# Multi-query attention on one core: score rounds planned by tiles that come free on the way, 27 weight places, two copies of V

## Chip, cores and metric

The kernel runs on one core of one Trainium2 chip. The metric is the time of one execution on the device in microseconds. A core has TensorE (PE; its weight loads are PEld), VectorE (DVE), ScalarE (ACT), GpSimd (POOL) and SyncE (SP), each with its own queue, which work beside each other and wait for one another through semaphores.

## What is computed

```python
q: (8, 1024, 16, 64)   k, v: (8, 1024, 64)   # batch, sequence, heads, head_dim
scores = q @ k^T / sqrt(64)                  # per batch and head; k and v are shared by the heads
weights = exp(scores - max); weights /= sum(weights)
out = weights @ v                            # (8, 1024, 16, 64)
```

## The kernel before

The work is cut into 1024 units of scores. A unit is 128 keys by two heads by 512 queries: two matmuls with 64 rows each (line 263), which write one of three score tiles in PSUM (two banks each). The scores lie with the keys on the partitions, so that the weights can be the stationary operand of the second product. A unit's number u runs over pairs of heads (64, eight in each batch), in each over two halves of the queries, and in each over eight blocks of keys.

Each unit is exponentiated in one of two ways. `kinds[u]` says in which:

- "A": ScalarE's exponential reads the score tile and writes 16-bit weights into one of N_WT places (line 276).
- "V": VectorE does it in passes over one of N_W3 triple places. `ve_bits` (line 283) reads the score tile and writes 16-bit integers that, read as 16-bit floats, are a first approximation. `ve_mantissa` (294), `ve_power` (304) and `ve_square` (315) make a mantissa, a power of two and a square from them, and a product of two of these is the third term. That product is shared: GpSimd takes the first columns of it, often in one or two pieces (`ve_cube`, line 319), and VectorE the rest (`ve_rest`, line 327). GpSimd's pieces are put beside passes of VectorE that read PSUM.

The value matmuls (line 396) multiply 128x128 blocks of weights with 65 columns of V (64 and one of ones, which gives the sum). An "A" unit needs eight, one for each of its 128x128 blocks; a "V" unit needs 24, since it has three terms, each with its own copy of V scaled by a coefficient (`vp`, three copies for each of two batches; `prep_v`, line 251, makes the scaled ones). Seven results share one of two PSUM banks; when they are complete VectorE takes the reciprocal of the sums (`inverse`, line 345) and multiplies (`finish`, line 354), and SyncE's queue stores them. q comes through GpSimd's DMA queue (line 166) as 16-bit and is turned by DMA transposes on SyncE's queue; the first q tiles are turned on TensorE.

All of this is ordered ahead of time by a planner, `plan()`, which runs on the host when the kernel is built. It keeps a clock for TensorE (`t_pe`), VectorE (`t_ve`), ScalarE (`t_act`) and GpSimd (`t_gp`), in nanoseconds, from constants such as T_PAIR (one unit of scores), T_MM (one value matmul), T_IN and T_OUT (going to scores and back), T_ACT and VE_COST. What it emits is only an order of instructions on each engine: the times in it bind nothing on the chip. There each engine goes through its own queue in order and waits for what its next instruction needs.

Scores are issued in rounds: TensorE does some units of scores, then value matmuls until the next round. `plan()` counts the score tiles that are free (`n_free`). If there are two or more it starts a round of so many. If there is one, it starts a round of one only where waiting for the next tile would leave ScalarE without work (`WAIT`, `NEAR`). `issue()` decides whether a unit goes to VectorE: only the second unit of a round may (`VSLOT = 1`), if VectorE's backlog is below `VE_SLACK`, the unit before did not go there, and the number of V units so far is below a share `RATE` of the units. `SAFE` is a margin that the planner adds to the time at which weights are ready before it orders their value matmul; `REST` is how many columns of the product may be left for VectorE; `LATE` and `NEXT` decide between VectorE's next passes.

Of the kernel before, what the change touches and what calls it, by code (L numbers as in the profile page):

```python
# [10 lines left out]
FP32 = mybir.dt.float32  # L11
FP16 = mybir.dt.float16
I32 = mybir.dt.int32
I16 = mybir.dt.int16
ALU = mybir.AluOpType
# [3 lines left out]

SUM_LO = 128.0  # L20
SUM_HI = 60000.0
C0 = 0.9833984375
C3 = 0.163818359375
CS = 2.1471603163479376
N_WT = 22
N_W3 = 8
N_M = 2
N_M2 = 3
T_PAIR = 214.0
T_IN = 96.0  # L30
T_OUT = 106.0
T_MM = 29.6
T_SCORE = 480.0
T_ACT = 917.0
ACT_DONE = 1110.0
MM_DONE = 270.0
VE_TAIL = 115.0
# [17 lines left out]
    "finish": 542.0,  # L55
}
ORDER = {"bits": 0, "inverse": 1, "finish": 2}
NEXT = {"bits": 0.0, "inverse": 0.0, "finish": 0.0}
MINC = 128
REST = 768  # L60
LATE = 500.0
VSLOT = 1
DEFER = 12
HOLD = 1400.0
VE_SLACK = 2500.0
V_END = 12
RATE = 0.235
NEAR = 2000.0
WAIT = -100.0
T_BITS = 1255.0  # L70
SAFE = 300.0


@with_exitstack
def attention_main(ctx, tc, q, k, v, out, flag):
# [13 lines left out]
    P = 128  # L89
    NKT = S // P  # L90
    QCH = 512
# [12 lines left out]
    consts = ctx.enter_context(tc.tile_pool(name="consts", bufs=1))  # L104
# [3 lines left out]
    wtp = ctx.enter_context(tc.tile_pool(name="wtp", bufs=1))  # L108
# [8 lines left out]
    ident16 = consts.tile([P, P], FP16, name="ident16")  # L117
    ones = consts.tile([P, 1], FP32, name="ones")
    rec_all = consts.tile([P, NG], FP32, name="rec_all")
    vps = [consts.tile([P, 3, NKT, 72], FP16, name=f"vp{i}") for i in range(2)]  # L120
    ok_all = consts.tile([P, B + GRP], FP32, name="ok_all")
    qf = consts.tile([P, NKT, P], FP32, name="qf")

    sc = {}
    ve = {}
# [3 lines left out]
    q16 = {}  # L129
# [21 lines left out]
        )  # L151

    def load_q_first(p):
        q16[("first", p)] = consts.tile([P, NKT, P], FP16, name=f"q16_first{p}")
        src = q[0, :, 2 * p : 2 * p + 2, :].rearrange("(c p) h d -> p c (h d)", p=P)
        if p:
            nc.gpsimd.dma_start(out=q16[("first", p)], in_=src)
            return
        for cs in (slice(0, NKT // 2), slice(NKT // 2, NKT)):
            nc.scalar.dma_start(out=qf[:, cs, :], in_=src[:, cs, :])  # L160
# [86 lines left out]

    def prep_v(b):
        vp = kv[b]["vp"]
        for i, ci in ((1, C0), (2, C3)):  # L250
            x = nc.vector.tensor_scalar(  # L251
                out=vp[:, i, :, 0:D], in0=vp[:, 0, :, 0:D], scalar1=ci, scalar2=None, op0=ALU.mult
            )
        return x
# [23 lines left out]
    def ve_bits(u, i):  # L278
        p, c, j = where(u)
        w3 = w3p.tile([P, 3, 2, QCH], FP16, tag=f"w3_{i}", name=f"we{p}_{c}_{j}")  # L280
        wt[u] = [(w3[:, 1], 0), (w3[:, 0], 1), (w3[:, 2], 2)]
        ve[u] = {"w3": w3}
        nc.vector.tensor_scalar(  # L283
            out=w3[:, 1].bitcast(I16),
            in0=sc.pop(u),
            scalar1=15.0 * 1024,
            scalar2=0.0,
            op0=ALU.add,
            op1=ALU.max,
        )  # L290

    def ve_mantissa(u, i):
        ve[u]["m"] = mp.tile([P, 2, QCH], FP16, tag=f"m{i}", name=f"m{u}")
        return nc.vector.tensor_scalar(  # L294
            out=ve[u]["m"].bitcast(I16),
            in0=ve[u]["w3"][:, 1].bitcast(I16),
            scalar1=0x3FF,
            scalar2=0x3C00,
            op0=ALU.bitwise_and,
            op1=ALU.bitwise_or,  # L300
        )

    def ve_power(u):
        return nc.vector.tensor_scalar(  # L304
            out=ve[u]["w3"][:, 0].bitcast(I16),
            in0=ve[u]["w3"][:, 1].bitcast(I16),
            scalar1=0x7C00,
            scalar2=None,
            op0=ALU.bitwise_and,
        )  # L310

    def ve_square(u, i):
# [154 lines left out]
    def plan():  # L467
        ops = []

        def emit(t, what, *args):  # L470
            ops.append((t, len(ops), what, args))

        t_pe = t_ve = t_act = t_gp = 0.0
        mode = "v"
        u = 0
        free = [0.0] * 3
# [31 lines left out]
        def slot():  # L508
            return min(range(3), key=lambda i: free[i])
# [7 lines left out]
        def backlog():  # L517

            t = sum(VE_COST[k] for k, _ in chain) + VE_COST["rest"] * len(left)
            return t + sum(VE_COST[k] for _, k, _, _ in evict)  # L520
# [24 lines left out]
        def vector_step(limit):  # L545
# [21 lines left out]
            if not urgent and (  # L567
                chain or left and (flush or left[next(iter(left))] <= REST or u - next(iter(left)) > DEFER)
            ):
                what, v = chain[0] if chain else ("rest", next(iter(left)))  # L570
                old = next(iter(left), None)
                if old is not None and (
                    left[old] <= REST
                    or what == "square"
                    and min(m2_used) == float("inf")
                    or u - old > DEFER
                ):
                    what, v = "rest", old
                s = t_ve
                if what == "mantissa":  # L580
                    s = max(s, ready[v, 0], min(m_used))
                elif what == "square":
                    s = max(s, live["s", v], min(m2_used))
                elif what == "rest":
                    s = max(s, squared[v] + VE_TAIL)
                if s >= limit:
                    return False
                share(s)
                s = max(s, lock)
                if what == "rest":  # L590
                    n = left.pop(v)
                    done = 0.0
                    if n:
                        emit(s, "rest", v, 2 * QCH - n)
                        t_ve = s + VE_FIX + n / 1.92
                        done = t_ve + VE_TAIL
                        behind, t_behind = ("rest", v), t_ve
                    ready[v, 2] = m2_used[live.pop(("m2", v))] = max(done, ready.get((v, "g"), 0.0))
                    return True
                chain.pop(0)  # L600
                t_ve = s + VE_COST[what]
                if what in ("prep_k", "prep_v", "check"):
                    emit(s, what, v)
                    behind, t_behind = (what, v), t_ve
                    return True
                done = t_ve + VE_TAIL
                behind, t_behind = (what, v), t_ve
                if what == "mantissa":
                    live["m", v] = hold(m_used, s)[0]
                    live["s", v] = done  # L610
                    emit(s, what, v, live["m", v])
                elif what == "power":
                    emit(s, what, v)
                    ready[v, 1] = done
                else:
                    m_used[live.pop(("m", v))] = done
                    live["m2", v] = hold(m2_used, s)[0]
                    emit(s, what, v, live["m2", v])
                    left[v] = 2 * QCH
                    squared[v] = t_ve  # L620
                return True
# [24 lines left out]
                    chain.append(("check", b))  # L646
            return True

        def issue(t, first):
            nonlocal u, t_act, made_v  # L650
            i = slot()
            s = max(t, free[i])
            to_v = (
                first
                and NKT <= u < STEPS - V_END
                and not todo
                and max(t_ve, s) + backlog() < s + T_SCORE + VE_SLACK
                and kinds.get(u - 1) != "V"
                and made_v < (u - NKT + 1) * RATE
                and min(w3_used) < s  # L660
            )
            if not to_v and min(wt_used) == float("inf"):
                return False
            kinds[u] = "V" if to_v else "A"
            made_v += to_v
            emit(s, "score", u, i)
            done = s + T_SCORE
            free[i] = float("inf")
            if to_v:
# [26 lines left out]
        while h < H or u < STEPS:  # L696
# [2 lines left out]

            while vector_step(t_pe):  # L700
                pass
            n_free = sum(f <= t_pe for f in free)
            go = n_free > 1
            if n_free == 1:
                other = sorted(late_free(i) for i in range(3))[1]
                go = max(other, t_pe) + T_IN + T_SCORE > t_act + WAIT and t_pe + NEAR >= t_act - T_IN - T_SCORE
            if u < STEPS and go:
                t = t_pe + (T_IN if mode == "v" else 0)
                k = 0
                while u < STEPS and k < n_free and issue(t, n_free > 1 and k == VSLOT):  # L710
                    t += T_PAIR
                    k += 1
                if k:
                    rounds += mode == "v"
                    mode = "s"
                    t_pe = t
                    continue
# [63 lines left out]
    with tc.manual_schedule():  # L781
# [6 lines left out]
        for c in range(NKT):  # L788
            load_q(0, c)
        for t in vps:  # L790
            for i, ci in enumerate((1.0, C0, C3)):
                nc.gpsimd.memset(t[:, i, :, D : D + 1], ci)
        nc.vector.tensor_copy(out=ident16, in_=ident)
        nc.vector.memset(ones, 1.0)
# [166 lines left out]
```

## Time and profile before

| | |
|---|---|
| time, median of 3 runs | 763.24 us (762.63 to 763.75) |
| the profiled execution's own time | 762.94 us |
| its span, from the first to the last instruction | 761.1 us |
| mean granted TensorE clock | 0.997 |
| units on ScalarE / on VectorE | 800 / 224 |
| value matmuls in the main loop | 11,712 |
| pieces of the product on GpSimd | 279 |

The span is what the profile's rows add up to; the profiled execution's own time is 1.84 us longer. In the profile, "Lnnn" is a line of the kernel. Names such as `sc`, `wt`, `we`, `ot` are tiles: scores, ScalarE's weights, VectorE's weights, results. A group's row has the number of its instructions, the time in which at least one of them ran, the mean length of one in ns, and the idle time of the engine in front of them. Records of instructions that follow each other on one engine overlap, so the mean length of one is more than its distance to the next.

### The profile page before, as it was taken

How to read it: one execution, taken by the hardware profiler on the slowest of the kernel's cores; microseconds unless marked ns; L12 is line 12 of the kernel's file. 1: busy time of each engine (PE TensorE's matmuls, PEld its weight loads, DVE VectorE, ACT ScalarE, POOL GpSimd, SP SyncE). 2: the span in 40 equal slices, each digit the busy share in tenths (PEclk: the TensorE clock that was granted, in tenths of full speed). 3: DMA queues.
4: the chain of work that ended last, by engine and by line, in shares of the span. 5: the costliest groups of instructions: out<-in, count | busy, mean ns of one | idle time of the engine just before them, and what ended most of it. 6: DMA issues, size and time to landing. Idle time of an engine off the chain costs nothing.

```text
span 761.1 us, 31746 instructions
## 1 busy us (share of the span) xinstructions
PE 746.3 (98%) x13858; PEld 480.7 (63%) x13858; DVE 728.8 (96%) x1474; ACT 747.5 (98%) x803; POOL 327.2 (43%) x364
## 2 busy tenths in 40 slices
PE   6999999999999999999999999999999999999996
PEld 3566666666666666666666666666666665666665
DVE  4999999999999999999999999999999999999994
ACT  7999999999999999999999999999999999999995
POOL 4644444443444344543444344434444334444440
PEclk9999999999999999999999999999999999999999
DMA  9964437663466525665446563467535565211112
GB/s 173 167 121 99 99 64 114 113 117 94 78 118 113 105 62 112 106 113 92 79 93 112 114 113 74 90 111 125 99 75 95 100 112 96 71 44 58 30 58 73
DMA packets 168926, 73.91 MB, mean 97 GB/s; under 512 B 94032, under 2 KB 161616, under 8 KB 168784
## 3 DMA queue, kind: packets, MB, share of 16 engines
q1 hardware_dynamic: 149152, 53.76, 32.7%
q0 software_dynamic: 18576, 17.57, 18.3%
q8 instruction: 109, 1.79, 1.1%
q10 hardware_dynamic: 1056, 0.52, 0.2%
q14 instruction: 33, 0.27, 0.1%
HBM read 37.75 MB, written 33.55 MB: 94 GB/s over the span
## 4 chain that ended last, share of the span: by engine, by line
ACT 54%; PE 42%; issue 3%; DMA 1%; DVE 1%
ACT wt L276 54%; PE ot L396 24%; PE sc L263 17%; DMA knat<-in_k_dram 0%; PE otl L420 0%; DMA out_dram<-osb 0%; DVE osb L354 0%; PE kps L200 0%; PE qps L216 0%; DVE k L191 0%; DVE rec_all L345 0%; DVE k2t L212 0%; PE cnt L837 0%; DVE okm L835 0%; DVE ok_all L443 0%
## 5 line engine op out<-in xcount | busy, mean ns | idle before, releaser
L276 ACT ACTIVATE wt<-sc 128x1024 f16<-128x1024 f32 x800 | 745.0, 1046 | 1.1 <-PE sc L263 0.9
L319 POOL TENSOR_TENSOR we<-we,mm 128x448 f16<-128x448 f16 (+4 forms) x279 | 281.9, 1010 | 409.2 <-DVE mm L315 214.4
L396 PE MATMUL ot<-vp,wt 128*128 128x65 f16 x6336 | 432.2, 194 | 0.0
L396 PE MATMUL ot<-vp,we 128*128 128x65 f16 x5376 | 432.2, 194 | 0.0
L396 PEld LDWEIGHTS <-wt 128*128 128x128 f16 x6336 | 317.4, 97 | 115.0 <-issue 115.0
L396 PEld LDWEIGHTS <-we 128*128 128x128 f16 x5376 | 316.1, 97 | 104.5 <-issue 103.4
L263 PE MATMUL sc<-qt,k2t 64*128 64x512 f16 x2048 | 354.3, 385 | 4.4 <-ACT wt L276 2.9
L283 DVE TENSOR_SCALAR we<-sc 128x1024 int16<-128x1024 f32 x224 | 272.5, 1217 | 8.7 <-PE sc L263 6.7
L315 DVE TENSOR_TENSOR mm<-m 128x1024 f16<-128x1024 f16 x224 | 151.8, 678 | 0.0
L263 PEld LDWEIGHTS <-k2t 64*128 64x128 f16 x2048 | 80.1, 93 | 48.5 <-issue 7.8
L294 DVE TENSOR_SCALAR m<-we 128x1024 int16<-128x1024 int16 x224 | 92.5, 413 | 0.2
L304 DVE TENSOR_SCALAR we<-we 128x1024 int16<-128x1024 int16 x224 | 92.5, 413 | 0.0
L354 DVE TENSOR_TENSOR osb<-ot,rec_all 128x448 f32<-128x448 f32 x146 | 89.2, 611 | 0.2
L327 DVE TENSOR_TENSOR we<-we,mm 128x576 f16<-128x576 f16 (+7 forms) x222 | 87.4, 394 | 0.0
L166 POOL DMA_DIRECT2D q<-in_q_dram x64 | 38.6, 606 | 5.5 <-issue 1.5
L345 DVE RECIPROCAL rec_all<-ot 128x7 f32<-128x7 f32 x146 | 28.7, 197 | 7.4 <-PE ot L396 6.8
L149 POOL DMA_DIRECT2D vp<-in_v_dram x8 | 7.2, 899 | 0.0
L251 DVE TENSOR_SCALAR vp<-vp 128x512 f16<-128x512 f16 x16 | 3.8, 279 | 2.2 <-DMA vp<-in_v_dram 2.2
L200 PE MATMUL kps<-ident,k 128*64 128x128 f16 x16 | 1.3, 314 | 4.4 <-DVE k L191 4.3
L234 DVE TENSOR_SCALAR k16d<-knat 128x1024 f16<-128x1024 f32 x7 | 4.7, 672 | 0.0
L229 DVE COPY qt<-qps 128x512 f16<-128x512 f16 (+1 forms) x2 | 1.1, 555 | 3.0 <-PE qps L216 3.0
L200 PEld LDWEIGHTS <-k 128*64 128x64 f16 x16 | 0.8, 158 | 4.6 <-DVE k L191 4.6
(30 smaller groups left out, 23.7 us busy)
## 6 DMA issues: line engine op xcount, KB each, us to landing
out_dram<-osb SPq DMA_DIRECT2D x109, 256.0 KB, 2.6
q<-in_q_dram POOLq DMA_DIRECT2D x56, 256.0 KB, 4.4
out_dram<-osb SPq DMA_DIRECT2D x38, 128.0 KB, 2.4
knat<-in_k_dram SPq DMA_DIRECT2D x7, 256.0 KB, 3.9
q<-in_q_dram POOLq DMA_DIRECT2D x8, 192.0 KB, 8.2
vp<-in_v_dram POOLq DMA_DIRECT2D x8, 128.0 KB, 5.8
qt<-q SPq DMA_TRANSPOSE x64, 4.8
qf<-in_q_dram ACTq DMA_DIRECT2D x2, 256.0 KB, 4.0
```

Source lines behind the costliest of these rows:

```text
L166: nc.gpsimd.dma_start(out=q16[(b, c)], in_=q[b, c * P : (c + 1) * P, h0:, :].rearrange("p h d -> p (h d)"),)
L263: nc.tensor.matmul(sc[u][:, hh, :], k2t[r : r + 64, j * P : (j + 1) * P], qt[b][r : r + 64, p % HP, c * QCH : (c + 1) * QCH], start=True, ...
L276: nc.scalar.activation(out=w, in_=sc.pop(u), func=EXP, scale=escale, bias=math.log(CS))
L283: nc.vector.tensor_scalar(out=w3[:, 1].bitcast(I16), in0=sc.pop(u), scalar1=15.0 * 1024, scalar2=0.0, op0=ALU.add, op1=ALU.max,)
L294: return nc.vector.tensor_scalar(out=ve[u]["m"].bitcast(I16), in0=ve[u]["w3"][:, 1].bitcast(I16), scalar1=0x3FF, scalar2=0x3C00, op0=ALU.b ...
L304: return nc.vector.tensor_scalar(out=ve[u]["w3"][:, 0].bitcast(I16), in0=ve[u]["w3"][:, 1].bitcast(I16), scalar1=0x7C00, scalar2=None, op0 ...
L315: return nc.vector.tensor_tensor(out=ve[u]["m2"], in0=m, in1=m, op=ALU.mult)
L319: x = nc.gpsimd.tensor_tensor(out=wu[:, lo:hi], in0=we[:, lo:hi], in1=mm[:, lo:hi], op=ALU.mult)
L327: return nc.vector.tensor_tensor(out=wu[:, lo:], in0=we[:, lo:], in1=mm[:, lo:], op=ALU.mult)
L345: nc.vector.reciprocal(out=rec_all[:, g0 : g0 + n], in_=o[:, 0:n, D])
L354: nc.vector.tensor_tensor(out=ob[:, i0 : i0 + n, :], in0=o[:, 0:n, 0:D], in1=rec.unsqueeze(2).broadcast_to([P, n, D]), op=ALU.mult,)
L396: nc.tensor.matmul(ots[g0][:, gg - g0, 0 : D + 1], w[:, hh, qb * P : (qb + 1) * P], kv[h // (HP * NCH)]["vp"][:, ci, u % NKT, 0 : D + 1], ...
```

## The change

The reference computation stays the same. VectorE's approximation gets other constants: its three terms need two copies of V, plain and times KAPPA, in place of three. The first q tiles, which had places of their own, now lie in places of the rings that are used late, and N_WT goes from 22 to 27. The planner's constants change, and its rule for rounds:

- A tile counts as free if it will be so when TensorE gets to it: the first at once (`FIRST`), the next by `t_in + n_free * T_PAIR + SOON`.
- In a round of two or more the unit for VectorE may be the first, where ScalarE does not need its unit at once (`at_v`).
- With one tile free, a round of one unit may go to VectorE alone, where ScalarE has work for over `AWAY` ns and VectorE's backlog is below `SLACK1`.

```diff
-C0 = 0.9833984375
-C3 = 0.163818359375
-CS = 2.1471603163479376
-N_WT = 22
+KAPPA = 1.5258396029178207
+CS = 3.2766468288976904
+N_WT = 27
-T_PAIR = 214.0
+T_PAIR = 215.5
-T_OUT = 106.0
-T_MM = 29.6
+T_OUT = 120.0
+T_MM = 30.2
-T_ACT = 917.0
+T_ACT = 905.0
-NEXT = {"bits": 0.0, "inverse": 0.0, "finish": 0.0}
+NEXT = {"bits": 100.0, "inverse": 0.0, "finish": 60.0}
-REST = 768
-LATE = 500.0
-VSLOT = 1
+REST = 500
+LATE = 2500.0
+EPS = 0.0
+AWAY = 1500.0
+SLACK1 = 300.0
+SOON = 0.0
+FIRST = 0.0
-VE_SLACK = 2500.0
+VE_SLACK = 1800.0
-RATE = 0.235
+RATE = 0.25
-WAIT = -100.0
+WAIT = 0.0
-SAFE = 300.0
+SAFE = 1000.0
...
-    vps = [consts.tile([P, 3, NKT, 72], FP16, name=f"vp{i}") for i in range(2)]
+    vps = [consts.tile([P, 2, NKT, 72], FP16, name=f"vp{i}") for i in range(2)]
-    qf = consts.tile([P, NKT, P], FP32, name="qf")
+    qf = (w3p.tile([P, 3, 2, QCH], FP16, tag=f"w3_{N_W3 - 1}", name="qf") ...)
...
-        q16[("first", p)] = consts.tile([P, NKT, P], FP16, name=f"q16_first{p}")
+        x = wtp.tile([P, 2, QCH], FP16, tag=f"wt{N_WT - 1 - p}", name=f"q16_first{p}")
+        q16[("first", p)] = x.rearrange("p h (c f) -> p (h c) f", f=P)
...
     def prep_v(b):
-        for i, ci in ((1, C0), (2, C3)):
+        for i, ci in ((1, KAPPA),):
...
     def ve_bits(u, i):
-        wt[u] = [(w3[:, 1], 0), (w3[:, 0], 1), (w3[:, 2], 2)]
+        wt[u] = [(w3[:, 1], 1), (w3[:, 0], 0), (w3[:, 2], 0)]
...
     def ve_mantissa(u, i):
-            scalar2=0x3C00,
+            scalar2=0x3800,
...
     def ve_power(u):
             scalar1=0x7C00,
-            scalar2=None,
+            scalar2=0x0201,
             op0=ALU.bitwise_and,
+            op1=ALU.bitwise_or,
...
-        def issue(t, first):
-            to_v = (
-                first
-                and NKT <= u < STEPS - V_END
+        def wants(s, slack):
+            return (
+                NKT <= u < STEPS - V_END
                 and not todo
-                and max(t_ve, s) + backlog() < s + T_SCORE + VE_SLACK
+                and max(t_ve, s) + backlog() < s + T_SCORE + slack
                 and kinds.get(u - 1) != "V"
                 and made_v < (u - NKT + 1) * RATE
                 and min(w3_used) < s
             )
+        def issue(t, slack):
+            to_v = slack is not None and wants(s, slack)
...
-            n_free = sum(f <= t_pe for f in free)
+            t_in = t_pe + (T_IN if mode == "v" else 0.0)
+            n_free = 0
+            for f in sorted(free):
+                if f > (t_in + n_free * T_PAIR + SOON if n_free else t_pe + FIRST):
+                    break
+                n_free += 1
             go = n_free > 1
+            slack = VE_SLACK if go else None
             if n_free == 1:
                 other = sorted(late_free(i) for i in range(3))[1]
                 go = max(other, t_pe) + T_IN + T_SCORE > t_act + WAIT and t_pe + NEAR >= t_act - T_IN - T_SCORE
+                if t_act > t_in + AWAY and wants(t_in, SLACK1):
+                    go = True
+                    slack = SLACK1
             if u < STEPS and go:
-                t = t_pe + (T_IN if mode == "v" else 0)
+                t = t_in
                 k = 0
-                while u < STEPS and k < n_free and issue(t, n_free > 1 and k == VSLOT):
-                    t += T_PAIR
+                at_v = int(n_free > 1 and t + T_PAIR + T_SCORE > t_act + EPS)
+                while u < STEPS and k < n_free and issue(t, slack if k == at_v else None):
+                    t = t_now + T_PAIR
                     k += 1
```

More of the change, by code (lines that the diff above doesn't have):

```diff
@@ L119, in attention_main @@
     rec_all = consts.tile([P, NG], FP32, name="rec_all")
-    vps = [consts.tile([P, 3, NKT, 72], FP16, name=f"vp{i}") for i in range(2)]
+    vps = [consts.tile([P, 2, NKT, 72], FP16, name=f"vp{i}") for i in range(2)]
     ok_all = consts.tile([P, B + GRP], FP32, name="ok_all")
-    qf = consts.tile([P, NKT, P], FP32, name="qf")
+    qf = (
+        w3p.tile([P, 3, 2, QCH], FP16, tag=f"w3_{N_W3 - 1}", name="qf")
+        .rearrange("p i h q -> p (i h q)")[:, 0 : 2 * NKT * P]
+        .bitcast(FP32)
+        .rearrange("p (c f) -> p c f", f=P)
+    )
     sc = {}
@@ L471, in emit @@
             ops.append((t, len(ops), what, args))
-        t_pe = t_ve = t_act = t_gp = 0.0
+        t_pe = t_ve = t_act = t_gp = t_now = 0.0
         mode = "v"
@@ L597, in vector_step @@
                         behind, t_behind = ("rest", v), t_ve
-                    ready[v, 2] = m2_used[live.pop(("m2", v))] = max(done, ready.get((v, "g"), 0.0))
+                    done = max(done, ready.get((v, "g"), 0.0), ready[v, 1])
+                    m2_used[live.pop(("m2", v))] = done
+                    ready[v, 2] = done
                     return True
@@ L647, in vector_step @@
             return True
-        def issue(t, first):
-            nonlocal u, t_act, made_v
-            i = slot()
-            s = max(t, free[i])
-            to_v = (
-                first
-                and NKT <= u < STEPS - V_END
+        def wants(s, slack):
+            return (
+                NKT <= u < STEPS - V_END
                 and not todo
-                and max(t_ve, s) + backlog() < s + T_SCORE + VE_SLACK
+                and max(t_ve, s) + backlog() < s + T_SCORE + slack
                 and kinds.get(u - 1) != "V"
@@ L661, in issue @@
             )
+        def issue(t, slack):
+            nonlocal u, t_act, made_v, t_now
+            i = slot()
+            s = max(t, free[i])
+            to_v = slack is not None and wants(s, slack)
             if not to_v and min(wt_used) == float("inf"):
@@ L664, in issue @@
             kinds[u] = "V" if to_v else "A"
-            made_v += to_v
+            if to_v:
+                made_v += 1
             emit(s, "score", u, i)
+            t_now = s
             done = s + T_SCORE
@@ L790, in attention_main @@
         for t in vps:
-            for i, ci in enumerate((1.0, C0, C3)):
+            for i, ci in enumerate((1.0, KAPPA)):
                 nc.gpsimd.memset(t[:, i, :, D : D + 1], ci)
```

## The prediction

> **What bounds the kernel now.** I read the engine line and the chain of the page first, then the busy time by stretches.
>
> ```profile
> PE 746.3 (98%) x13858; PEld 480.7 (63%) x13858; DVE 728.8 (96%) x1474; ACT 747.5 (98%) x803; POOL 327.2 (43%) x364
> ...
> ACT 54%; PE 42%; issue 3%; DMA 1%; DVE 1%
> ```
> ```profile
> 0.00:20.00 20.00, 13.77 (x139) 6.85 (x140) 9.37 (x22) 15.26 (x17) 9.67 (x25) 0.91 1.21 174
> ...
> 300.00:400.00 100.00, 99.88 (x1882) 64.81 (x1880) 98.43 (x200) 100.00 (x109) 43.52 (x48) 1.00 0.56 100
> ...
> 740.00:761.10 21.10, 15.18 (x360) 11.71 (x356) 11.01 (x32) 12.39 (x14) 1.58 (x2) 0.96 0.23 66
> ```
>
> The columns of the stretches are length, then busy time of PE, PEld, DVE, ACT, POOL, then clock, DMA share and GB/s. Three engines are over 98% busy in the middle. A busy ACT or PE may still be waiting, because instructions overlap in the records; the chain, which passes between ACT and PE, is the first hint. So I ask what each engine needs when it waits for nobody, ScalarE first.
>
> ```profile
> L276 ACT ACTIVATE wt<-sc 128x1024 f16<-128x1024 f32 x800 | 745.0, 1046 | 1.1 <-PE sc L263 0.9
> ```
> ```profile
> L276 ACT ACTIVATE wt<-sc x800: 1018/1023/1236, 7.0 to 751.3; 128x1024 f16<-128x1024 f32 x160
> ```
> ```profile
> 14.67 12.61 ACT wt L276 x14
> ...
> 97.81 4.56 ACT wt L276 x5
> ...
> 145.22 3.74 ACT wt L276 x4
> ```
>
> The starts of the 800 exponentials run from 7.0 to 751.3 us, one every (751.3 - 7.0) / 799 = 0.931 us. The last three rows are pieces of the chain. The longest has 14 in 12.61 us, 0.901 each; the others 0.912 and 0.935. ScalarE alone would need 800 x 0.901 = 721 us where it takes 745. Some 24 us are waits, shorter than the overlap of two records (1.046 - 0.931 = 0.115 us), so that the waits view does not see them.
>
> TensorE next: the timeline (start and length in us, count at the end), a line of the waits (us in total, times, longest) and the groups.
>
> ```profile
> 300.46 0.39 PE L263 MATMUL sc<-qt,k2t 64*128 64x512 f16 x2
> ...
> 300.78 0.27 PE L396 MATMUL ot<-vp,wt 128*128 128x65 f16 x3
> ...
> 301.27 0.20 PE L396 MATMUL ot<-vp,we 128*128 128x65 f16 x1
> ...
> 301.40 0.39 PE L263 MATMUL sc<-qt,k2t 64*128 64x512 f16 x2
> ...
> 302.35 0.61 PE L263 MATMUL sc<-qt,k2t 64*128 64x512 f16 x4
> ...
> 302.89 0.24 PE L396 MATMUL ot<-vp,wt 128*128 128x65 f16 x2
> ...
> 304.12 0.19 PE L396 MATMUL ot<-vp,wt 128*128 128x65 f16 x1
> ...
> 304.24 0.61 PE L263 MATMUL sc<-qt,k2t 64*128 64x512 f16 x4
> ```
> ```profile
> PEld L396 <- issue: 218.4, 740, 0.4
> ```
> ```profile
> L396 PE MATMUL ot<-vp,wt 128*128 128x65 f16 x6336 | 432.2, 194 | 0.0
> L396 PE MATMUL ot<-vp,we 128*128 128x65 f16 x5376 | 432.2, 194 | 0.0
> L263 PE MATMUL sc<-qt,k2t 64*128 64x512 f16 x2048 | 354.3, 385 | 4.4 <-ACT wt L276 2.9 <-DVE we L283 0.8
> ```
>
> A score unit is two of these matmuls. Between the rounds that start at 300.46 and 301.40 lie one unit and 17 value matmuls (the L396 rows between, of which the first and the last are shown, added up), in 0.94 us; from 302.35 to 304.24 two units and 41, in 1.89 us. A further unit costs 0.61 - 0.39 = 0.22. So a value matmul costs (1.89 - 0.94 - 0.22) / 24 = 0.030 us, and what is left of the first, 0.94 - 0.22 - 17 x 0.030 = 0.20 us, is paid per round: going from value matmuls to scores and back. The waits view has 740 such returns. Counted through the trace by its score rows there are 744 rounds: 475 of one unit, 264 of two, 4 of three and one long one at the start. Sum for TensorE: 1024 x 0.22 = 225, 11,712 x 0.0305 = 357, 744 x 0.20 = 149, together 731 of the 745 us of the exponentials; rounding and the start hold the rest. It idles 4.4 us in front of scores. So **TensorE is the pacemaker**, and a fifth of its time is the changing between two kinds of matmul. ScalarE's hidden waits are waits for it.
>
> VectorE, one full cycle from its timeline:
>
> ```profile
> 299.88 0.67 DVE L315 TENSOR_TENSOR mm<-m 128x1024 f16<-128x1024 f16 x1
> ...
> 300.48 1.21 DVE L283 TENSOR_SCALAR we<-sc 128x1024 int16<-128x1024 f32 x1
> ...
> 301.62 0.19 DVE L345 RECIPROCAL rec_all<-ot 128x7 f32<-128x7 f32 x1
> ...
> 301.73 0.41 DVE L294 TENSOR_SCALAR m<-we 128x1024 int16<-128x1024 int16 x1
> ...
> 302.06 0.61 DVE L354 TENSOR_TENSOR osb<-ot,rec_all 128x448 f32<-128x448 f32 x1
> ...
> 302.59 0.34 DVE L327 TENSOR_TENSOR we<-we,mm 128x384 f16<-128x384 f16 x1
> ...
> 302.86 0.41 DVE L304 TENSOR_SCALAR we<-we 128x1024 int16<-128x1024 int16 x1
> ...
> 303.19 0.68 DVE L315 TENSOR_TENSOR mm<-m 128x1024 f16<-128x1024 f16 x1
> ```
> ```profile
> DVE we L283 <- PE sc L263: 6.7, 27, 0.5
> ```
>
> From square to square it is 3.31 us, of which the eviction (0.11 + 0.53) is 0.64: a VectorE unit costs 2.67 us here. VectorE is busy 728.8 us, and at the two ends it cannot work for 20 - 9.37 = 10.6 and 21.1 - 11.01 = 10.1 us. That makes 749.5 of 761.1, so it idles only 11.6 us in the middle. It is the second bound, close behind.
>
> **The change part by part.** *Rounds.*
>
> ```profile
> 14.72 0.61 PE L263 MATMUL sc<-qt,k2t 64*128 64x512 f16 x2
> ...
> 741.69 0.39 PE L263 MATMUL sc<-qt,k2t 64*128 64x512 f16 x2
> ```
>
> A round now counts a tile as free if it comes free by the time TensorE reaches it: the second up to T_IN + T_PAIR = 0.31 us after the decision. The rows show the case: the round at 301.40 has one unit, and the tile of the VectorE pass that began at 300.48 is free at 300.48 + 1.21 = 301.69, 0.29 us later; it is refilled at 302.35. Counted through the trace, 179 of the 475 one-unit rounds have such a tile (177 of them VectorE's), the first and the last of which are these two. Next to them the round that follows has two units, so pairing earlier does not delete a round each time: it lets the third tile go to work up to 0.94 us sooner, for a second ScalarE unit or the next VectorE one. A VectorE unit now comes with 744 / 224 = 3.3 rounds and 4.57 units. In twos throughout that would be 2.3. I take 90 rounds fewer, half of the 179. Bounds: 179 fewer, which is -36 us on TensorE, and 112 more (rival below), +22 us. At 90 it is 90 x 0.20 = 18 us off TensorE, to 743 us of span with today's ends.
>
> *The planner's clock.* It sets only the order, but the order is good only if it keeps time. For 17 values and one unit the old constants give 96 + 214 + 17 x 29.6 + 106 = 919 ns, the new ones 96 + 215.5 + 17 x 30.2 + 120 = 945; the rows say 940. For 41 and two units: 1844, 1885 and 1890. The old plan thinks TensorE 2% faster than it is, hence tiles that had long been free. T_ACT goes from 917 to 905, beside 901 to 912 in the chain's pieces. No instruction's cost hangs on it.
>
> *ScalarE.* With 18 us off TensorE its hidden waits shrink. I take 0.905 us for a spacing: 800 x 0.905 = 724, and with its ends (7.0 before; 761.1 - 751.3 - 1.0 = 8.8 after) 740 us. Bounds are 0.901 and today's 0.931: 737 and 761. The Trainium skill has a rule against this (ScalarE: Activation LUTs, section "What ACT_TABLE_LOAD costs"): an ACTIVATE with immediate scale and bias takes 186 ns + 0.833 ns per element, and back-to-back ones overlap by about 93 ns. By it, as an estimate, 1024 elements cannot follow each other faster than 946 ns, and 800 of them with today's ends would need 773 us, so feeding ScalarE better could bring nothing. The trace disagrees: 14 in 12.61 us.
>
> *VectorE's share and its work.* Cap RATE rises from 0.235 to 0.25, the slack falls from 2500 to 1800, and V may go first or alone. One unit more on VectorE is -0.93 for ScalarE, +2.67 for VectorE and +16 x 0.0305 = +0.49 for TensorE; with VectorE at 749.5 there is no room for many. I keep 224 (218 to 232). Per unit the passes are the same five.
>
> ```profile
> L294 DVE TENSOR_SCALAR m<-we 128x1024 int16<-128x1024 int16 x224 | 92.5, 413 | 0.2
> L304 DVE TENSOR_SCALAR we<-we 128x1024 int16<-128x1024 int16 x224 | 92.5, 413 | 0.0
> ...
> L251 DVE TENSOR_SCALAR vp<-vp 128x512 f16<-128x512 f16 x16 | 3.8, 279 | 2.2 <-DMA vp<-in_v_dram 2.2
> ...
> L319 POOL TENSOR_TENSOR we<-we,mm 128x512 f16<-128x512 f16 x93 | 107.3, 1154 | 175.4 <-DVE mm L315 99.3 <-PE sc L263 31.3 <-DVE m L294 20.7
> L319 POOL TENSOR_TENSOR we<-we,mm 128x448 f16<-128x448 f16 x92 | 94.7, 1029 | 145.3 <-DVE mm L315 87.8 <-PE sc L263 35.0 <-DVE m L294 13.2
> ...
> L327 DVE TENSOR_TENSOR we<-we,mm 128x576 f16<-128x576 f16 x87 | 38.4, 442 | 0.0
> ...
> L327 DVE TENSOR_TENSOR we<-we,mm 128x288 f16<-128x288 f16 x31 | 9.5, 305 | 0.0
> ```
>
> The power pass gets a second operation (or 0x0201). L294 has two already and costs the same 413 ns as L304 with one: nothing. A third copy of V less: eight passes of 279 ns, 2.2 us off VectorE. REST falls from 768 to 500, so VectorE may no longer take the usual 576-column remainder at once, but waits for GpSimd to have a second piece. (442 - 305) / 288 is 0.48 ns a column; 87 remainders cut by 128 columns are 5 us, and the bound is none (GpSimd already has 185 pieces of 448 or 512 for 224 L283 passes, so its places are mostly taken) to 12. I take 3. Price: w3 and m2 tiles are held longer, behind which the next square stands on VectorE.
>
> *Waits and places.* SAFE goes from 300 to 1000: a value matmul is ordered 0.7 us later behind its weights. That is 0.7 / 0.93, less than one more weight tile; five more are there. Without them TensorE, which runs in order, would have scores standing behind a missing weight tile, and ScalarE behind those. The first q tiles now lie in weight places 25 and 26: the 26th exponential comes 25 x 0.93 = 23 us after 7.0, long after they are read. The constants for V's ones and the two-copy layout change no count of matmuls: 8 for a ScalarE unit, 24 for a VectorE unit. All nothing.
>
> **Sum, against the profiled execution** (span 761.1, time 762.94, so 1.8 around it; 0.3 under the median 763.24). TensorE 743, ScalarE 740, VectorE 749.5 - 2.2 - 3 = 744. VectorE is last. Three engines this close cannot all run without waiting; of VectorE's 11.6 us of idle middle I keep a third, 4. Span 748, time **750.0**. By the Trainium skill's ScalarE spacing it would stay over 763.
>
> **Rivals.** *More rounds instead of fewer (slower).* A VectorE unit may now have a round alone when ScalarE is booked 1.5 us ahead, and 219 of the 264 two-unit rounds are a ScalarE unit with a VectorE one behind (by their readers in the trace). If 112 of these split and 60 pairs are won elsewhere, it is 52 rounds more, 10.4 us on a TensorE that has 0.12 us idle in 100: 773. It decides from the first round over 744. For it: the rows show no spare TensorE time. Against: the tile that the pairing needs is there 179 times. Chance 0.17.
>
> *ScalarE has no slack.* If the short runs of 0.901 are the exception and 0.931 is its pace beside all its neighbours, 800 units keep 761 of span; a few units moved to VectorE give -4: time 759 to 763. The Trainium skill's ScalarE rule would have it so. Against: the pieces of 14 and of 5. Chance 0.12.
>
> *The pairs come but stall.* The second tile is counted on to the nanosecond, and TensorE stands in order if it is late; today it idles 4.4 us there. If half of the rounds' gain goes so, TensorE is at 752 and the time is 754 to 758. Chance 0.13.
>
> **How the numbers follow.** The forecast (741 to 754) has 0.58. About 0.2% (1.5 us) is what a measurement here can tell from no change. Faster: 0.58 + 0.13 + 0.05 of the second rival = 0.76; same 0.05 from it; slower 0.17 + 0.02 = 0.19. The range goes from 740 (ScalarE at 0.901 with its ends, plus 1.8) to 767 (20 rounds more); the likeliest case alone is 741 to 754.
>
> **What would show it.** Right: under 690 returns to value matmuls (740 now), exponentials spaced under 0.915 us, TensorE no longer 99.9% busy in the middle, VectorE's share 218 to 232 units, eight V passes. Wrong: returns over 740; spacing still 0.93 with fewer returns (the second rival); several tens of us of idle in front of L263 on PE (the third); or over 235 or under 215 VectorE units, which my sum does not hold.

## The result and the profile after

The changed kernel takes 755.41 us (755.11 to 756.33, 4 runs) where the kernel before took 762.98 in the same runs: a ratio of 0.9901, 95% interval 0.9884 to 0.9919, 7.6 us less. The forecast was 750.0, in a range of 740 to 767. The way and the order of size were right; 5.4 of the 13 us forecast did not come, and the time lies 1.4 us outside the forecast's likeliest case (741 to 754). The profiled execution took 756.33 with a span of 754.6.

Of the changed kernel, the engine line and the chain of the page:

```profile
PE 737.3 (98%) x13826; PEld 490.6 (65%) x13826; DVE 719.4 (95%) x1452; ACT 738.5 (98%) x805; POOL 332.8 (44%) x328
...
PE 90%; ACT 6%; DVE 2%; issue 1%; DMA 0%; ACTq 0%
```

Its groups:

```profile
L285 ACT ACTIVATE wt<-sc 128x1024 f16<-128x1024 f32 x802 | 736.0, 1208 | 2.2 <-PE sc L272 2.0
...
L406 PE MATMUL ot<-vp,wt 128*128 128x65 f16 x6352 | 423.6, 194 | 0.0
L406 PE MATMUL ot<-vp,we 128*128 128x65 f16 x5328 | 417.4, 194 | 0.0
...
L272 PE MATMUL sc<-qt,k2t 64*128 64x512 f16 x2048 | 349.8, 388 | 6.9 <-ACT wt L285 6.0
L292 DVE TENSOR_SCALAR we<-sc 128x1024 int16<-128x1024 f32 x222 | 270.5, 1219 | 11.7 <-PE sc L272 8.3
...
L260 DVE TENSOR_SCALAR vp<-vp 128x512 f16<-128x512 f16 x8 | 2.2, 277 | 1.7 <-DMA vp<-in_v_dram 1.7
```

Its waits and its stretches (columns as before):

```profile
PEld L406 <- issue: 169.6, 636, 0.8
```
```profile
0.00:20.00 20.00, 14.59 (x122) 6.41 (x123) 7.92 (x18) 15.33 (x17) 9.44 (x23) 1.00 1.12 176
20.00:40.00 20.00, 18.49 (x269) 10.86 (x268) 18.89 (x36) 18.79 (x21) 8.67 (x11) 0.83 0.89 141
...
300.00:400.00 100.00, 100.00 (x1925) 67.56 (x1922) 98.50 (x202) 100.00 (x110) 44.53 (x39) 1.00 0.59 100
```

TensorE now goes back to its value matmuls 636 times, where it was 740: the rounds fell from 744 to 637 (264 of one unit, 368 of two). The units are split 802 to 222 between ScalarE and VectorE. The middle stretch holds 110 exponentials where it held 109. By chain and busy shares TensorE still seems to set the time: 90% of the chain, 100.00 us busy of 100. The experiments say otherwise.

The row that shows why is ScalarE's own timeline from 40 to 735 us, which merges exponentials that leave the engine no gap. First the kernel before, then the changed one:

```profile
39.25 696.38 ACT L276 ACTIVATE wt<-sc 128x1024 f16<-128x1024 f32 x747
```
```profile
39.12 697.04 ACT L285 ACTIVATE wt<-sc 128x1024 f16<-128x1024 f32 x760
```

Such a row runs from the first start to the last end, so one instruction's own length (the groups' means, 1.05 and 1.21) comes off before dividing. Before it is (696.38 - 1.05) / 746 = 0.932 us an exponential, after it is (697.04 - 1.21) / 759 = 0.917. That 0.917 is taken as the engine's own pace; the experiments test it. Taken through the trace from each end to the next, the middle half of the changed kernel's distances lies at 916 to 917 ns, and the median is 917 before as well. Above 917 the distances add up to 12.1 us in the kernel before, of which 11.5 are exponentials whose scores TensorE, busy throughout, brought late, and to 2.3 us in the changed one. So ScalarE's account is:

- before: first end at 8.0, 799 x 0.917 = 732.7, waits 12.1, tail after the last end 8.7: 761.5 (span 761.1);
- after: 7.9, 801 x 0.917 = 734.5, waits 2.3, tail 10.2: 754.9 (span 754.6).

### The profile page after: what moved, and what is told of

Same layout as the page of the kernel before. It is cut to its first block, busy times and chain, and to the rows that moved or that the text cites. A ratio compares the mean times of both kernels' runs of the same rounds, so it can differ in the third digit from the quotient of the medians.

```text
span 754.6 us, 31778 instructions
## 1 busy us (share of the span) xinstructions
PE 737.3 (98%) x13826; PEld 490.6 (65%) x13826; DVE 719.4 (95%) x1452; ACT 738.5 (98%) x805; POOL 332.8 (44%) x328
## 4 chain that ended last, share of the span: by engine, by line
PE 90%; ACT 6%; DVE 2%; issue 1%; DMA 0%; ACTq 0%
PE ot L406 52%; PE sc L272 37%; ACT wt L285 6%; DVE we L292 1%; DMA qf<-in_q_dram 0%; DVE osb L364 0%; DVE mm L325 0%; PE otl L430 0%; PE qps L225 0%; DVE m L303 0%; DVE we L337 0%; DVE we L313 0%; DVE rec_all L355 0%; ACT q_first L826 0%; ACT qt L238 0%
## 5 line engine op out<-in xcount | busy, mean ns | idle before, releaser
L285 ACT ACTIVATE wt<-sc 128x1024 f16<-128x1024 f32 x802 | 736.0, 1208 | 2.2 <-PE sc L272 2.0
L329 POOL TENSOR_TENSOR we<-we,mm 128x736 f16<-128x736 f16 (+7 forms) x245 | 287.7, 1174 | 400.6 <-DVE mm L325 120.0
L406 PE MATMUL ot<-vp,wt 128*128 128x65 f16 x6352 | 423.6, 194 | 0.0
L406 PE MATMUL ot<-vp,we 128*128 128x65 f16 x5328 | 417.4, 194 | 0.0
L406 PEld LDWEIGHTS <-we 128*128 128x128 f16 x5328 | 310.9, 98 | 79.1 <-issue 78.8
L272 PE MATMUL sc<-qt,k2t 64*128 64x512 f16 x2048 | 349.8, 388 | 6.9 <-ACT wt L285 6.0
L272 PEld LDWEIGHTS <-k2t 64*128 64x128 f16 x2048 | 95.8, 93 | 81.6 <-issue 28.1
L337 DVE TENSOR_TENSOR we<-we,mm 128x288 f16<-128x288 f16 (+10 forms) x216 | 83.8, 388 | 0.0
L260 DVE TENSOR_SCALAR vp<-vp 128x512 f16<-128x512 f16 x8 | 2.2, 277 | 1.7 <-DMA vp<-in_v_dram 1.7
```

The costliest lines, as they stand in the source:

```text
L272: nc.tensor.matmul(sc[u][:, hh, :], k2t[r : r + 64, j * P : (j + 1) * P], qt[b][r : r + 64, p % HP, c * QCH : (c + 1) * QCH], start=True, ...
L285: nc.scalar.activation(out=w, in_=sc.pop(u), func=EXP, scale=escale, bias=math.log(CS))
L329: x = nc.gpsimd.tensor_tensor(out=wu[:, lo:hi], in0=we[:, lo:hi], in1=mm[:, lo:hi], op=ALU.mult)
L337: return nc.vector.tensor_tensor(out=wu[:, lo:], in0=we[:, lo:], in1=mm[:, lo:], op=ALU.mult)
L406: nc.tensor.matmul(ots[g0][:, gg - g0, 0 : D + 1], w[:, hh, qb * P : (qb + 1) * P], kv[h // (HP * NCH)]["vp"][:, ci, u % NKT, 0 : D + 1], ...
```

## The experiments

Each gives the median, and the ratio to the kernel before run beside it, with its 95% interval. ScalarE's waits are the sums above 917 ns from end to end, taken from the profiled execution.

| kernel | us | ratio, interval | rounds | ScalarE units | ScalarE's waits, us |
|---|---|---|---|---|---|
| before | 762.98 | | 744 | 800 | 12.1 |
| changed | 755.41 | 0.9901 (0.9884 to 0.9919) | 637 | 802 | 2.3 |
| changed, a third of V units' matmuls out | 755.52 | 0.9899 (0.9883 to 0.9916) | 637 | 802 | 1.7 |
| before, the same out | 751.72 | 0.9850 (0.9833 to 0.9866) | 744 | 800 | 1.1 |
| changed, old count | 761.06 | 0.9977 (0.9965 to 0.9988) | 722 | 800 | 8.5 |
| before, new count | 761.78 | 0.9980 (0.9970 to 0.9989) | 677 | 800 | 10.1 |
| changed, old clock | 761.15 | 0.9966 (0.9953 to 0.9978) | 617 | 801 | 10.0 |
| changed, V unit second | 756.44 | 0.9902 (0.9886 to 0.9919) | 655 | 803 | 3.8 |
| changed, T_ACT 917 | 755.24 | 0.9881 (0.9864 to 0.9898) | 628 | 802 | 3.5 |
| clock from traces, 226 V units | 753.75 | 0.9869 (0.9852 to 0.9885) | 639 | 798 | 4.3 |
| clock from traces, 225, quiet start | 751.32 | 0.9849 (0.9832 to 0.9867) | 670 | 799 | 1.3 |
| before, new count and clock | 758.62 | 0.9941 (0.9924 to 0.9957) | 698 | 801 | 5.4 |
| changed, 22 places | 760.69 | 0.9973 (0.9961 to 0.9985) | 655 | 800 | 9.9 |
| changed, SAFE 300 and REST 768 | 755.41 | 0.9893 (0.9876 to 0.9911) | 648 | 803 | 2.2 |

**Who sets the time?** Both kernels with less work on TensorE, in their own order:

```diff
         w, ci = wt[u][i]
+        if i == 1:
+            return
         nc.tensor.matmul(
```

> The changed kernel in the same order on every engine, but the eight value matmuls of each VectorE unit's second term (the power of two) are left out: 222 x 8 = 1776 matmuls of 0.031 us, 55 us less for TensorE; the output lacks that term. Theory S (ScalarE is the last bound now; its exponentials end 0.917 us apart whatever feeds them): 802 x 0.917 = 735 us plus its ends 6.9 and 10.2, plus 1.8 = 754; without the 2 us of waits that are left, 752 to 755, no more than 3 us less than the changed kernel's 755.4. Theory T (TensorE still paces, and half of what the fewer rounds saved went into stalls inside rounds): TensorE becomes free, the time falls by more than 6 us, below 749.

> The same on the kernel before: 224 x 8 = 1792 value matmuls left out, 55 us less for TensorE, same order; the output lacks that term. Theory S: only ScalarE's waits go, 800 x 0.917 = 733.6 plus ends 15.7 plus 1.8 = 751, so 750 to 753, and exponentials that end 0.917 us apart. The prediction's pace of 0.905 from the pieces of the chain would give 724 + 15.7 + 1.8 = 741.5. Theory T says nothing against 741 to 751 here, but wants the light version of the changed kernel to fall as far.

The changed kernel stays at 755.52: 55 us of TensorE's work taken out, and nothing gained. The kernel before falls to 751.72. Engine line, chain and ScalarE's timeline of the light changed kernel, then of the light kernel before:

```profile
PE 719.5 (95%) x12050; PEld 452.6 (60%) x12050; DVE 719.2 (95%) x1452; ACT 738.3 (98%) x805; POOL 332.6 (44%) x328
...
ACT 54%; PE 38%; issue 5%; DVE 1%; DMA 0%; ACTq 0%
```
```profile
39.55 696.02 ACT L285 ACTIVATE wt<-sc 128x1024 f16<-128x1024 f32 x759
```
```profile
ACT 78%; PE 17%; issue 4%; DMA 1%; DVE 1%
```
```profile
38.90 697.03 ACT L276 ACTIVATE wt<-sc 128x1024 f16<-128x1024 f32 x760
```

Whatever feeds it, ScalarE makes 759 or 760 exponentials in this stretch. That settles it for the theory that ScalarE is the last bound (S), and against the one that TensorE still is (T). It also settles that TensorE was the pacemaker before, that its removal was worth 11 us at most there, and that the pace behind it is 0.917, not the 0.905 that would have given 741.5. TensorE's busy time falls by only 17.8 us in the light changed kernel (737.3 to 719.5): nearly all of the other 37 us turn up between the units of one round, where TensorE now stands 57.3 us for score tiles instead of 20.4 (measured from start to start, above 226 ns, the median in the kernel before). The records of neighbouring matmuls mostly cover such a stand, so it counts as busy. The chain of waits named TensorE at 90% in a kernel that does not feel a third of its V units' matmuls going: with two engines a few hundredths apart it follows whichever came last each time.

**Which part of the change does it?** The way of counting, undone in the changed kernel and done alone in the kernel before:

```diff
-                if f > (t_in + n_free * T_PAIR + SOON if n_free else t_pe + FIRST):
+                if f > t_pe:
```

> The changed kernel with the old way of counting alone: a tile is free if it is so at the decision. The order has 722 rounds in place of 637 and 224 VectorE units in place of 222. Theory S: 85 rounds x 0.19 = 16 us more for TensorE, which makes it the pacemaker again, ScalarE's waits are back: 759 to 763. Theory T: the 13 us of stalls inside rounds go as the 16 us come: 756 to 759.

> The kernel before with the new way of counting alone (the second tile by T_IN + T_PAIR after the decision), all constants as before. The order has 677 rounds in place of 744, 224 VectorE units. Theory S: 67 x 0.19 = 13 us off TensorE is about ScalarE's 11.7 us of waits: 751 to 755. Theory T: half of it is lost in stalls: 756 to 758. If the planner's clock or the other constants carried the gain, it stays over 760.

Undone it costs 5.8 us (0.9977 against 0.9901), as theory S had it. TensorE is again short of time, and ScalarE's waits for it appear openly, that is, long enough for the waits view to list them. Stretch and waits of the changed kernel with the old count:

```profile
300.00:400.00 100.00, 100.00 (x1881) 65.09 (x1878) 98.97 (x200) 99.48 (x109) 47.04 (x50) 1.00 0.49 98
```
```profile
PEld L406 <- issue: 215.4, 718, 0.6
...
ACT wt L285 <- PE sc L272: 4.1, 13, 0.7
```

Done alone it brings 1.5 us (0.8 to 2.3 by its interval), where theory S expected 8 to 12: 67 rounds fewer, and ScalarE waits 10.1 us all the same. That expectation fell, and what came is the last of the three: it stays over 760. The count needs another part beside it. The next ones undo the planner's clock, and the unit for VectorE at the head of its round:

```diff
-T_PAIR = 215.5
+T_PAIR = 214.0
-T_OUT = 120.0
-T_MM = 30.2
-T_ACT = 905.0
+T_OUT = 106.0
+T_MM = 29.6
+T_ACT = 917.0
```

> The changed kernel with the four constants of the planner's clock of before (T_PAIR, T_OUT, T_MM, and T_ACT 917). The order has 617 rounds, 20 fewer than the changed kernel's, and 223 VectorE units. Theory C (a clock that runs ahead of TensorE makes an order in which TensorE is late at each round, and ScalarE waits for it, however few the rounds): 10 us of ScalarE's waits come back, as in the kernel before with the new count: 760 to 764. Theory R (the number of rounds decides, together with the other constants): 801 x 0.917 plus ends, 753 to 756.

```diff
-                at_v = int(n_free > 1 and t + T_PAIR + T_SCORE > t_act + EPS)
+                at_v = 1
```

> The changed kernel with VectorE's unit always second in its round, as before. The order has 655 rounds and 221 VectorE units. If putting it first is worth only its rounds and units: 803 x 0.917 = 736.4 plus ends, one exponential more than the changed kernel's, 755 to 757.5. If being first is what keeps VectorE or ScalarE fed: 759 or more.

```diff
-T_ACT = 905.0
+T_ACT = 917.0
```

> The changed kernel with T_ACT at 917 in place of 905, the distance at which exponentials were seen to end. 628 rounds, still 802 units for ScalarE. Theory S (ScalarE is the last bound, 802 x 0.917): no more than 2 us gained, 753 to 756. If the wrong 905 cost something, the order fits better and the 2.3 us of waits that the changed kernel has left (2.0 of them in its first 40 us) go: 752.5 to 754. If the 905 helped by driving scores early: 757 or more.

The old clock gives 761.15 with 617 rounds, the fewest of all: theory C's 760 to 764, not theory R's. Its waits:

```profile
PEld L406 <- issue: 192.0, 614, 0.8
...
PE sc L272 <- ACT wt L285: 15.2, 42, 0.5
...
ACT wt L285 <- PE sc L272: 3.6, 6, 0.7
```

TensorE waits for tiles 15.2 us in the open (6.0 in the changed kernel) and is late for ScalarE as well: of ScalarE's 10.0 us, 3.8 fall in the first 40 us, and most of the rest are exponentials whose scores came late from a TensorE that was busy. The reading is that an order made for a TensorE 2% faster puts rounds where they do not fit, on either side. T_ACT alone, back at 917, moves nothing that the intervals can tell (755.24), so the cost lies with the three TensorE constants, though T_ACT together with them was not run apart. VectorE's unit always second gives 756.44, the first of its expectations; its ratio (0.9902 against 0.9901) shows no loss, so being first in the round is not what the change lives by.

The rest of the change, tried from both sides:

> The kernel before with two parts of the change: the new way of counting and the four constants of the planner's clock. 698 rounds, 223 VectorE units, 22 places, VectorE's unit second, SAFE, REST, LATE, NEXT, VE_SLACK, RATE and WAIT as before. Each part alone gave 2 us or less. If the two together are the change: 801 x 0.917 plus ends, 754 to 757. If the other constants or the places carry a part of it: 758 to 762.

```diff
-N_WT = 27
+N_WT = 22
```

> The changed kernel with 22 weight places instead of 27. The order has 655 rounds, 224 VectorE units, 20 of them alone in a round. If the places cost nothing (my step of the prediction): two exponentials fewer than the changed kernel, 752 to 755.5. If the planner runs out of places and ScalarE stands for them: 757 to 762.

Count and clock together bring the kernel before to 758.62, 4.5 of the 7.6 us, which is the second expectation: the places or other constants carry a part. With 22 places the changed kernel takes 760.69, though it has two exponentials fewer; 20 VectorE units then go alone. Its waits:

```profile
PE sc L272 <- ACT wt L285: 9.1, 24, 0.5
ACT wt L285 <- PE sc L272: 7.0, 19, 0.7
```

So three parts, each undone alone, cost 5.0 to 5.8 us of the 7.6 (by their ratios: clock 5.0, places 5.5, count 5.8). They do not add up: ScalarE's waits go only when nothing makes TensorE late. The clock alone and the places alone, in the kernel before, were not run, nor were NEXT, LATE, VE_SLACK, RATE, WAIT and the two copies of V apart from the rest. With SAFE at 1000 the five further places are needed; whether they are with SAFE at 300 was not run on its own.

**The start, and a faster version.** The changed kernel has 2.0 of its 2.3 us of waits in the first 40 us. Its scores there:

```profile
22.17 0.39 PE L272 MATMUL sc<-qt,k2t 64*128 64x512 f16 x2 [0.18 <-ACT wt L285]
23.09 0.39 PE L272 MATMUL sc<-qt,k2t 64*128 64x512 f16 x2 [0.52 <-ACT wt L285]
24.00 2.44 PE L272 MATMUL sc<-qt,k2t 64*128 64x512 f16 x8 [0.52 <-ACT wt L285]
26.68 1.04 PE L272 MATMUL sc<-qt,k2t 64*128 64x512 f16 x4
```

From 22 to 26.4 us the order has no value matmul; up to 24 us TensorE mostly stands. From 24.0 to 30.9 us the granted clock is 0.50 (0.83 over 20 to 40 us). In that time two units take 1.04 us in place of 0.61, and ScalarE's longest wait in this stretch is for such scores, 1.06 us:

```profile
30.66 9.51 ACT L285 ACTIVATE wt<-sc 128x1024 f16<-128x1024 f32 x10 [1.06 <-PE sc L272]
```

Two orders of my own, and one with two constants of before:

> The changed kernel with a planner's clock of what the traces show (T_PAIR 221, T_IN 98, T_OUT 96, T_MM 31.1, T_ACT 917) and with its other thresholds chosen so that the order has 226 VectorE units in 639 rounds, VectorE's unit mostly second. Theory S: 798 exponentials, 4 x 0.917 = 3.7 us less than the changed kernel's: 750 to 753. Theory V (VectorE, whose ends leave it 13.7 us of idle time, is the next bound): four units more are 4 x 2.67 = 10.7 us, nearly all of it, so stalls take the gain: 754 to 757.

> As the kernel with 226 VectorE units (clock from the traces), but with thresholds chosen so that its order leaves TensorE less idle time between 10 and 40 us: 225 VectorE units in 670 rounds, 13 of them a VectorE unit alone. Theory G (in the first 40 us TensorE stands without ordered value matmuls, the granted clock then falls to half, and late scores cost ScalarE 2 to 4 us): ScalarE's waits there fall under 1 us, 799 x 0.917 = 732.7 plus ends and 1.8: 750 to 752.5, faster than the kernel with 226. If the start's waits are not from that idle time, or if 31 more rounds make TensorE late again: 754 or more.

> The changed kernel with SAFE 300 and REST 768 as before, which order value matmuls earlier and shorten TensorE's idle time after 15 us; 648 rounds, 221 VectorE units. Theory G: the 2.0 us of waits in the first 40 us fall under 1, for one exponential more (0.9): 754 to 755.5, and the granted clock stays at 1.00 from 20 to 100 us. If SAFE at 300 makes TensorE stand before weights that are late: 757 or more.

The edit that the first two share, beside thresholds chosen by the planner's own end time (for the quiet start also by its idle time of TensorE from 10 to 40 us), and that of the third:

```diff
-T_PAIR = 215.5
-T_IN = 96.0
-T_OUT = 120.0
-T_MM = 30.2
-T_ACT = 905.0
+T_PAIR = 221.0
+T_IN = 98.0
+T_OUT = 96.0
+T_MM = 31.1
+T_ACT = 917.0
...
```
```diff
-REST = 500
+REST = 768
-SAFE = 1000.0
+SAFE = 300.0
```

226 VectorE units give 753.75, between the two expectations. By the ratios that is 2.4 us less than the changed kernel where four units are worth 3.7; ScalarE waits 1.9 us more in the first 40 us (3.9 in place of 2.0). The quiet start gives **751.32**, 4.0 us faster than the changed kernel (0.9849 against 0.9901), as theory G had it. Its stretches:

```profile
0.00:20.00 20.00, 13.61 (x138) 6.67 (x138) 9.07 (x21) 15.27 (x17) 9.67 (x23) 0.91 1.13 177
20.00:40.00 20.00, 19.66 (x337) 12.57 (x335) 19.90 (x40) 20.00 (x23) 12.12 (x12) 1.00 1.11 154
300.00:400.00 100.00, 99.97 (x1910) 67.23 (x1907) 99.51 (x205) 99.97 (x110) 49.84 (x44) 1.00 0.62 100
```

From 20 to 40 us the clock stays at 1.00 and 337 matmuls run where the changed kernel had 269. The half clock is not gone: it comes earlier (0.91 from 0 to 20 us, as in the kernel before) and is shorter (3.4 us in place of 6.8). ScalarE's waits are 0.5 us in the first 40 us, and VectorE is at 99.5% in the middle. Of the 5.7 us between the two profiled spans, three exponentials fewer are about 2.8, a shorter tail 2.3 and fewer waits 1.0; so the start's waits (2.0 to 0.5) are the smaller part of it. VectorE is not the last bound of the changed kernel either: with three and four units more it takes less time. SAFE and REST alone did not do it: 755.41 lies in theory G's range, but its signs did not come, with a clock of 0.91 in that stretch and 1.9 us of waits left. That the half clock, and not the lack of ordered value matmuls itself, costs the 2 to 4 us is therefore likely but not shown.

## Why the prediction was right, and where it was off

- **TensorE as the pacemaker before:** right. Less work for it frees the 11 to 12 us of ScalarE's waits, and nothing else.
- **Rounds:** 90 fewer forecast, 107 measured, both within the bounds; that they lie so close is in part luck. The 179 rounds were read generously: 0.31 us counts from the decision, which is 0.10 us before the scores start, and so counted the trace has 134 of them. (The tile of the round at 301.40 comes 0.39 us after the decision.) The count alone took off 67, the rest came with the other constants and rules. The price of 0.20 us a round was right too: in the distances from unit to unit within rounds and from kind to kind, a round less is 0.19.
- **ScalarE's pace:** the term that failed. I had 0.905 us from a piece of the chain, 14 exponentials in 12.61 us, and divided by 14. The chain's next rows show what such a piece measures:

```profile
27.27 0.06 issue
27.33 0.77 ACT wt L276
```

  The piece runs from the first start at 14.67 to the start of the 15th exponential at 27.33. So 14 is the number of distances from start to start. These are 903 to 904 ns after the first (920), while the ends come 915 to 917 apart: each record begins a little longer before its predecessor ends, and their lengths grow from 1.02 to 1.18 us. The starts run ahead of the ends, and the pace is that of the ends. The same stretch in ScalarE's own timeline of the kernel before has a row that can be divided:

```profile
14.67 25.77 ACT L276 ACTIVATE wt<-sc 128x1024 f16<-128x1024 f32 x28 [0.23 <-PE sc L263]
```

  (25.77 - 1.02) / 27 = 0.917. On 800 units the 0.012 us are 9.6 us: ScalarE at 740 should have been 750, and it, not VectorE, was last. T_ACT in the kernel before had the right 917. For the same reason the 24 us of waits that the forecast gave ScalarE were 12.1. With 802 units, 2.3 us of waits and a tail 1.4 us longer than before that is the measured span.
- **The rival "ScalarE has no slack":** half right. ScalarE is the bound of the changed kernel, but at 0.917, not at 0.931; in the kernel before it had 12 us of waits to lose. The Trainium skill's rule (ScalarE: Activation LUTs, "What ACT_TABLE_LOAD costs"), which I set aside for the 14 in 12.61, gave 946 ns as an estimate: 3% too long, as my 905 was 1.3% too short. It pointed at the right engine.
- **The rival "the pairs come but stall":** the stalls came. Between units of one round TensorE stood 6.9 us above the usual 226 ns before and 20.4 after. But they cost nothing: the light changed kernel is no faster. That its 754 to 758 held the time is luck: the time is there for another reason.
- **The rival "more rounds":** did not happen. The order of the changed kernel has no VectorE unit alone in a round.
- **The planner's clock "at nothing":** wrong as I put it. No instruction's cost hangs on it, and the time does: 5.0 us. My own rows, 919 against 940 and 945, held the reason.
- **Places and SAFE "all nothing":** not borne out as parts. Without the places it is 5.5 us; I had named who would wait without them (scores behind a missing place, ScalarE behind those), but gave it no price. Whether both together are nothing stays open, since 22 places with SAFE at 300 were not run in the changed kernel.
- **VectorE:** 222 units in 218 to 232, and eight passes at L260, as forecast. The smaller remainders are worth 2.8 us (L327's 87.4 us of busy time became 83.8 at L337, of which 0.8 are the two units fewer) where I took 3. VectorE's busy time and its two ends are 719.4 + 21.5 = 741 us, below ScalarE's account.
- **The signs:** returns, VectorE's share and the V passes came as written. Two did not: ends lie 917 ns apart, not under 915, and TensorE is still 100% busy in the middle. The second was no sign of who is last, since TensorE's stands inside a round count as busy.
- **The range:** its lower end of 740 does not follow from its own terms; 737 of span and 1.8 are 739.

## What to carry to other kernels

When two engines are both at 98%, neither busy share nor the chain says which is last. Take each engine's pace from the ends of instructions that follow without a gap, multiply by its count and add its two ends; then take work off one of them in an unchanged order and see whether the time moves. A schedule made ahead of time is worth its clock: constants 2% short for TensorE cost here about as much as the rule that they served (5.0 against 5.8 us). Parts that gain only together look worthless one by one, so undo them one by one as well.

## What the runs showed of the hardware

- Exponentials of 128 x 1024 from PSUM to 16-bit SBUF end 917 ns apart (916 to 917 for the middle half), though their records last 1.02 us when fed late and 1.2 when fed early (mean 1208 ns at L285). Starts came 903 to 904 ns apart while the engine caught up, so here the ends give the pace and the starts do not.
- TensorE's granted clock fell to 0.50 from 24.0 to 30.9 us, some 2 us into a stretch of sparse work early in the run (0.83 over 20 to 40 us), and the same scores then took 1.04 us for 0.61. The Trainium skill (TensorE: Matmul & The Clock Gate, Part 1) tells of a half-rate state after an idle window of some 3.4 us, free-running and so different from run to run. The trace agrees with the half rate; but TensorE was sparse, not idle, from 22 to 26 us: no idle time there was longer than 0.52 us. The four executions of the changed kernel had mean clocks of 0.993 (span 754.6) and 0.997 (753.3 to 753.8).
